# Attention for two heads at a time: one exponential for both, products with v in blocks of two key tiles, maxima by one transpose, reciprocals in two parts

## The chip, the core and the metric

The kernel runs on one core of one Trainium2 chip. The metric is the device time of one execution in microseconds. PE is the matrix engine (PEld its weight loads), DVE, ACT and POOL are the vector, scalar and general engines, SP issues most DMAs.

## The reference

Two blocks stand one behind the other. The first has two layers of attention over 512 latent tokens and 256 context tokens, width 1024, heads of 64. Each layer has three mixers of eight heads: A attends to all keys, B to a neighbourhood with a bias, C to a window with a sink. Layer 0 also attends from the context tokens; layer 1 doesn't. The second block (a recurrent and a convolution mixer, a conformer, two mixtures of experts) is not touched.

```python
def block(qi):                                   # mixer A; B and C alike, with bias, mask, sink
    s = jnp.einsum('bqhgd,bkhd->bhgqk', qi, k_all)
    p = softmax_f32(s, v_all.dtype)
    return jnp.einsum('bhgqk,bkhd->bqhgd', p, v_all)
...
mod = c_silu @ ada_w + ada_b                     # modulation, for every layer
hx = rmsnorm(x, norm_w) * (1 + scale[:, None, :]) + shift[:, None, :]
ux = jnp.concatenate([ya, yb, yc_], axis=-1) * jax.nn.silu(px[9])
x = x + gate[:, None, :] * (ux @ w_out)
```

## The kernel before

`layer` runs six groups per layer: mixer A's (or C's) two, B's two, C's (or A's) two; a group has four heads in two pairs. `pair` calls `attend` once for the latent queries and, in layer 0, once for the context queries: 24 latent attends and 12 of the context. While a group's pairs run, the projections for the next group (`proj_tok`, `proj_feat`, whose matmuls are lines 159 to 161 and 362 to 364) and the gate of the last are open too. A scheduler sets one fixed order of instructions for each engine from the order of the code and priorities; each engine runs its own in that order.

An attend has these steps, for the pair's two heads i = 0 and 1.

- **Maxima.** Scores with queries on the partitions (lines 698 to 725), reduced along the keys on DVE into `mt`. A matmul with one column of `mt` as weights (line 738), one for each head and each 128 queries, lays them along a row in bank `pr`. ACT copies the row into the operand `q2` (line 740), so that the second score matmul also subtracts the maximum.
- **Scores.** For each tile of 128 keys and each head, `st` writes the transposed scores into a bank "s" of 128x512 (two matmuls, lines 757 and 760; the masks of C between, line 759). There are two such banks.
- **Exponentials.** ACT writes P of 128x512 from the bank (line 813; 788 for the context; for mixer B DVE adds the bias first, line 842, and the exponential is line 843). P has four buffers (`PB`).
- **Sums.** `add` sums P over the key tiles into `acc` of that head (line 776), by turns on DVE and POOL, so that head 0 has DVE and head 1 POOL where a tile makes one add for each.
- **Products with v.** After each key tile `avm` (line 763) multiplies with v, 64 columns of the array for each head, into one bank `av` of 128x512: head 0 on partitions 0 to 63, head 1 on 64 to 127. P and v are full fp32, and each such matmul has two records in the trace. A and C have six key tiles of up to 512 queries (in C 256 or 384 for four of them); B has two of 512 and four of 256.
- **Normalising.** `reciprocals` sums four heads' `acc` over the partitions (line 865) and takes reciprocals on DVE (line 867) into `rs`; `normalise` spreads them with the 0/1 matrix `bsel` (line 876, fp32) and multiplies `y`.

Beside this, `fill` (called once at the end of every projection) advances `adaln_v`, which works out the modulation of later layers on DVE from weights in the ring (lines 243 and 245, 512 or 1024 wide) and sums over the partitions on PE (line 253).

Of the kernel before, what the change touches and what calls it, by code (L numbers as in the profile page):

```python
# [12 lines left out]
F32 = mybir.dt.float32  # L13
# [4 lines left out]
ALU = mybir.AluOpType  # L18
# [30 lines left out]
class K:  # L49
# [179 lines left out]
    def adaln_v(self, z, wsrc, a, b, nv, bias, mod, tmp):  # L229
# [4 lines left out]
        n = 1024 // nv  # L234
        for c0 in range(a, b, n):
            acc = self.t(tmp, [128, 1024], tag="adr", bufs=1)[:].rearrange("p (v n) -> p v n", v=nv)
            for k0 in range(0, 8, 2 * nv):
                w = self.wload(kview(wsrc[k0 * 128:(k0 + 2 * nv) * 128, c0:c0 + n]), 2 * nv, n)
                for k in range(2 * nv):
# [6 lines left out]
                if k0 + 2 * nv < 8:  # L246
                    yield 1
# [100 lines left out]
    def proj_tok(self, wsrc, nk, tiles, evac):  # L348
# [17 lines left out]
        self.fill(1)  # L366

    def proj_feat(self, wsrcs, x, segs, evac, nb=2, kind="b"):
# [22 lines left out]
        self.fill(1)  # L391


    R0 = 6

    def first_block(self):
        nc, A = self.nc, self.A
        with ExitStack() as es:
# [9 lines left out]
            self.bsel = load("bsel", [128, 2, 128])  # L408
# [6 lines left out]
            with self.rings(self.R0, 3), self.banks(a=2, f=2, b=3, x=1):  # L415
                xs = self.new_x()
                with self.pool("fl") as fl, self.pool("ec") as ec:
                    z1, c1 = self.cvec(ec, "cv1", fp)
# [84 lines left out]
    def layer(self, l, eh, norm=None):  # L503
# [5 lines left out]
        with eh, ExitStack() as es:  # L509
            with self.banks(m=2, s=2, av=1, b=3):  # L510
# [172 lines left out]
    def attend(self, mx, seg, hpair, q1, q2, k1, k2, vf, y, l):  # L683
# [7 lines left out]
        mt = self.t(ap, [128, 2, 4], tag="mt", bufs=3)  # L691
# [38 lines left out]
        if mx == 0 and lat:  # L730
            nc.vector.tensor_reduce(mt[:], mp[:], op=ALU.max, axis=AX.X)
# [19 lines left out]
        if lat:  # L751
            acc = [self.t(ap, [128, 512], tag="acc", bufs=4) for _ in range(2)]
        else:
            acc = [self.t(ap, [128, 256], tag="accc", bufs=2) for _ in range(2)]
# [10 lines left out]
        first = [None, None]  # L765
# [1289 lines left out]
```

## Time and profile before

| | |
|---|---|
| Median of three runs | 3079.18 us (3076.28 to 3086.53) |
| The profiled execution's own time | 3082.83 us |
| Its span | 3080.8 us |
| Busy in the span: PE, DVE | 2760.5 us (90%), 1514.0 us (49%) |
| ACT, POOL | 923.3 us (30%), 815.7 us (26%) |
| Mean granted clock of PE | 0.952 |

The durations used are from the one profiled execution. A busy time counts overlapping instructions once. The end of a matmul is modelled, so that a row of PE can reach beyond the start of the next; the distance of two starts is the better price. Where a wait is put down to an engine, it is the one whose signal came last.

### The profile page before, as it was taken

The numbers are of one execution on the slowest core, as the hardware profiler recorded it, in microseconds if no ns is written. First come the engines' busy times: TensorE is split into PE (matmuls) and PEld (weight loads), VectorE is DVE, ScalarE is ACT, GpSimd is POOL, SyncE is SP. The second block draws the span as 40 slices with busy tenths as digits, with TensorE's granted clock in tenths as the row PEclk, the third lists the DMA queues.
The fourth block names the chain that finished last, engine by engine and source line by source line (L and its number), as shares of the span: only waits on it lengthen the run. The fifth ranks groups of instructions, "written<-read, shape, count | busy, mean of one in ns | idle before, by whom it ended". The sixth has DMA issues, their size and how long they took to land.

```text
span 3080.8 us, 36122 instructions
## 1 busy us (share of the span) xinstructions
PE 2760.5 (90%) x14014; PEld 1717.2 (56%) x14014; DVE 1514.0 (49%) x2793; ACT 923.3 (30%) x1651; POOL 815.7 (26%) x689
## 2 busy tenths in 40 slices
PE   6889899999899999999998877998888997998887
PEld 2486567776588666765676764433333665333332
DVE  5886664656625645786356773222124663221222
ACT  3434343443423453434335321101002232110101
POOL 2243233332333334343534660000001431000000
PEclk8999899999899999999999888999999998999999
DMA  9632024222253214421331338999996574999996
GB/s 285 210 124 62 22 87 133 90 73 66 73 164 120 76 54 145 137 89 55 116 97 58 103 116 345 420 421 420 421 420 244 154 271 192 420 420 420 420 421 273
DMA packets 225306, 634.26 MB, mean 206 GB/s; under 512 B 12559, under 2 KB 141591, under 8 KB 175728
## 3 DMA queue, kind: packets, MB, share of 16 engines
q1 hardware_dynamic: 213344, 597.62, 51.7%
q0 software_dynamic: 7312, 25.96, 2.5%
q10 hardware_dynamic: 4480, 8.39, 0.7%
q8 instruction: 110, 1.80, 0.3%
q14 instruction: 60, 0.49, 0.1%
HBM read 612.87 MB, written 19.14 MB: 205 GB/s over the span
## 4 chain that ended last, share of the span: by engine, by line
PE 28%; DMA 19%; DVE 5%; POOL 2%; ACT 2%; issue 1%; SPq 0%; DVEq 0%; ACTq 0%; POOLq 0%
DMA mr<-in_exp_w_dram 10%; PE b L1859 10%; DMA mq<-in_exp_w_dram 8%; PE b L159 4%; PE b L161 4%; PE b L160 3%; PE av L763 1%; PE b L209 1%; PE b L1844 1%; PE q L275 1%; DVE lh L1262 0%; PE s L757 0%; DMA scratch<-sb 0%; PE b L324 0%; DVE f L1473 0%
## 5 line engine op out<-in xcount | busy, mean ns | idle before, releaser
L154 POOL TENSOR_TENSOR wl<-ring,wh 128x512 fp32r<-128x512 f32 x304 | 417.3, 1377 | 676.1 <-ACT wh L153 658.0
L153 ACT CAST wh<-ring 128x512 fp32r<-128x512 f32 x304 | 187.4, 620 | 505.9 <-PE b L161 366.6
L1859 PE MATMUL b<-mr,xs 128*64 128x512 f32 x1216 | 283.7, 617 | 37.2 <-DMA mr<-in_exp_w_dram 28.7
L159 PE MATMUL b<-hh,wh 128*128 128x512 f32 (+1 forms) x800 | 294.9, 369 | 3.0 <-DVE sc L621 3.0
L160 PE MATMUL b<-hh,wl 128*128 128x512 f32 (+1 forms) x800 | 290.6, 363 | 1.3 <-POOL wl L154 1.3
L161 PE MATMUL b<-hl,wh 128*128 128x512 f32 (+1 forms) x800 | 289.4, 363 | 0.1
L1859 PE MATMUL b<-mq,xs 128*64 128x512 f32 x832 | 189.2, 604 | 25.2 <-DMA mq<-in_exp_w_dram 16.8
L1859 PEld LDWEIGHTS b<-mr,xs 128*64 128x64 f32 x1216 | 90.1, 141 | 216.6 <-issue 154.6
L1801 POOL DMA_INDIRECT xg<-scratch,ix x16 | 15.5, 967 | 728.0 <-DVE ix L1795 687.5
L763 PE MATMUL av<-P,kv 128*64 128x512 f32 (+2 forms) x672 | 191.8, 518 | 3.0 <-ACT P L813 1.8
L1859 PE MATMUL b<-mr,sb 128*64 128x512 f32 x704 | 159.4, 597 | 18.5 <-DMA mr<-in_exp_w_dram 18.3
L159 PEld LDWEIGHTS b<-hh,wh 128*128 128x128 f32 x800 | 153.3, 192 | 32.4 <-issue 5.6
L160 PEld LDWEIGHTS b<-hh,wl 128*128 128x128 f32 x800 | 153.2, 192 | 26.9 <-issue 4.3
L161 PEld LDWEIGHTS b<-hl,wh 128*128 128x128 f32 x800 | 152.6, 191 | 25.0 <-issue 4.5
L362 PE MATMUL b<-wh,hh 128*128 128x256 f32 x512 | 148.9, 291 | 2.1 <-DVE kb L1160 1.3
L813 ACT ACTIVATE P<-s 128x512 f32<-128x512 f32 (+2 forms) x224 | 116.7, 551 | 113.8 <-PE s L760 110.0
L363 PE MATMUL b<-wl,hh 128*128 128x256 f32 x512 | 148.3, 290 | 0.3 <-POOL wl L154 0.3
L364 PE MATMUL b<-wh,hl 128*128 128x256 f32 x512 | 147.8, 289 | 0.4 <-DVE hl L345 0.4
L1883 DVE TENSOR_TENSOR yl<-yl,b 128x512 f32<-128x512 f32 x32 | 22.0, 688 | 254.1 <-PE b L1859 254.1
L1859 PEld LDWEIGHTS b<-mq,xs 128*64 128x64 f32 x832 | 60.2, 138 | 146.2 <-issue 101.6
L776 POOL TENSOR_TENSOR acc<-acc,P 128x256 f32<-128x256 f32 (+2 forms) x96 | 99.5, 1039 | 118.2 <-ACT P L813 94.2
L757 PE MATMUL s<-q1l,k 128*128 128x512 f32 (+2 forms) x288 | 113.2, 403 | 2.1 <-DVE sc L802 1.6
(564 smaller groups left out, 5681.4 us busy)
## 6 DMA issues: line engine op xcount, KB each, us to landing
mr<-in_exp_w_dram SPq DMA_DIRECT2D x120, 2048.0 KB
mq<-in_exp_w_dram SPq DMA_DIRECT2D x72, 2048.0 KB
ring<-in_w_mod_dram SPq DMA_DIRECT2D x96, 512.0 KB
ring<-in_w_in_dram SPq DMA_DIRECT2D x96, 512.0 KB
ring<-in_ada_w_dram SPq DMA_DIRECT2D x48, 512.0 KB
ring<-in_w_out_dram SPq DMA_DIRECT2D x32, 512.0 KB
bias<-in_BS_dram POOLq DMA_DIRECT2D x16, 512.0 KB, 3.8
bias<-in_BT_dram POOLq DMA_DIRECT2D x16, 512.0 KB, 4.0
```

Of the source, the lines that this page charges most:

```text
L153: nc.scalar.copy(h, src)
L154: nc.gpsimd.tensor_tensor(l, src, h.bitcast(F32), op=ALU.subtract)
L159: m(out, w[0], x[0], start=start, stop=False, skip_group_check=chk)
L160: m(out, w[1], x[0], start=False, stop=False, skip_group_check=chk)
L161: m(out, w[0], x[1], start=False, stop=stop, skip_group_check=chk)
L362: m(o, hh, wh[:, kk, :], start=(k == 0 and i % 2 == 0), stop=False, skip_group_check=True)
L363: m(o, hh, wl[:, kk, :], start=False, stop=False, skip_group_check=True)
L364: m(o, hl, wh[:, kk, :], start=False, stop=stop, skip_group_check=True)
L757: mm(ps, k1[i][:, kt * 128:kt * 128 + 128], q1[i][:, a:b], start=True, stop=False)
L763: mm(av[64 * i:64 * i + 64, a:b], vf(i, kt), P, start=start, stop=stop)
L813: nc.scalar.activation(p[:, :w], ps[:, :w], AF.Exp)
L1859: mm(ps[hf][64 * e:64 * e + 64, :], lhs(k, e), wt[:, e, k2, hf * 512:hf * 512 + 512], start=k == 0, stop=k == 7)
```

## The change

- **One activation for both heads.** `bank2` gives a tile "d" of 128x1024, two banks of PSUM, one for each head. It has one buffer, in place of the two banks "s". The exponential is one instruction of up to 128x1024 into a P of that size; P has two buffers (`PB` = 2), and `acc` holds both heads, 2 x 512. In mixer B the bias is still added head by head.
- **Sums for both heads in one add**, in turn on DVE and POOL along one chain.
- **Products in blocks.** `products` takes two key tiles and issues four matmuls, the later tile first, heads in turn.
- **Maxima.** `mt` is a view of one of three buffers `mw` of 128x100 that are set to zero once per layer; head 1's columns lie 32 behind head 0's. One transpose per 128 queries brings 96 columns to 96 partitions; the rows are 0 and 32.
- **Reciprocals in two parts.** `bsel` is rounded once (0 and 1), `rs` is split into a rounded part `rh` (ACT) and the rest `rl` (POOL), and `normalise` adds two matmuls of rounded operands in place of one in fp32.
- **Modulation.** `adaln_v` works in units of half the width, and `fill` is called for two (`FILL` = 2) where it was one; in the second block it is one again.

```diff
+    def bank2(self):
+        return self.t(self.psum, [128, 1024], tag="d", bufs=self.caps["d"])[:].rearrange("p (i n) -> p i n", i=2)
...
-        n = 1024 // nv
+        n = 512 // nv
+        nk = 2 * nv
...
-        self.fill(1)
+        self.fill(self.FILL)
...
-            with self.banks(m=2, s=2, av=1, b=3):
+            with self.banks(m=2, d=1, av=1, b=3):
...
+                    self.mw, self.nmw = self.chunks(ap, "mw", 3, 100), 0
+                    for w in self.mw:
+                        nc.gpsimd.memset(w[:], 0.0)
...
-        mt = self.t(ap, [128, 2, 4], tag="mt", bufs=3)
+        mw = self.mw[self.nmw % len(self.mw)]
+        self.nmw += 1
+        mt = mw[:, 0:64].rearrange("p (i t) -> p i t", i=2)[:, :, 0:4]
...
-        for i in range(2):
-            for t in range(nq):
-                mm(pr[64 + 32 * i:65 + 32 * i, t * 128:t * 128 + 128], mt[:, i, t:t + 1], self.ident[:], start=True, stop=True)
+        for t in range(nq):
+            nc.tensor.transpose(pr[0:96, t * 128:t * 128 + 128], mw[:, t:t + 96], self.ident[:])
         for i in range(2):
-            nc.scalar.copy(q2[i][64:65, :], pr[64 + 32 * i:65 + 32 * i, :n])
+            nc.scalar.copy(q2[i][64:65, :], pr[32 * i:32 * i + 1, :n])
...
-        def avm(i, kt, P, a, b, start, stop):
-            mm(av[64 * i:64 * i + 64, a:b], vf(i, kt), P, start=start, stop=stop)
+        def products(items, start=False, stop=False):
+            todo = [(i, *x) for x in reversed(items) for i in range(2)]
+            for j, (i, kt, P, a, b) in enumerate(todo):
+                mm(av[64 * i:64 * i + 64, a:b], vf(i, kt), P[:, i, :], start=start and j < 2, stop=stop and j >= len(todo) - 2)
...
+        def add(P, a, b, first=None):
+            o = acc[:, :, a:b]
+            self.nadd += 1
+            eng = nc.vector if self.nadd % 2 else nc.gpsimd
+            eng.tensor_tensor(o, o if first is None else first, P, op=ALU.add)
...
-        def tile1(kt, a, b, mask=(), start=False, stop=False):
-            Ps = []
-            w = b - a
+        def tile1(kt, a, b, mask=()):
+            ps = self.bank2()[:, :, :b - a]
             for i in range(2):
-                ps = self.bank("s")
-                st(i, kt, ps[:, :w], a, b, mask)
-                p = newP()
-                nc.scalar.activation(p[:, :w], ps[:, :w], AF.Exp)
-                add(i, p[:, :w], a, b)
-                Ps.append(p)
-            for i in range(2):
-                avm(i, kt, Ps[i][:, :w], a, b, start, stop)
+                st(i, kt, ps[:, i, :], a, b, mask)
+            P = newP()[:, :, :b - a]
+            nc.scalar.activation(P, ps, AF.Exp)
+            return kt, P, a, b
+
+        t4, t5 = tile1(4, 0, N), tile1(5, 0, N)
+        add(t5[1], 0, N, t4[1])
+        products([t4, t5], start=True)
...
-        rs = self.t(self.ap, [128, 512], tag="rs", bufs=1)
-        self.nc.vector.reciprocal(rs[:], ps[:])
-        return rs
+        rs = self.scratch()
+        self.nc.vector.reciprocal(rs, ps[:])
+        rh, rl = [self.t(self.ap, [128, 512], F32R, tag=tag, bufs=1) for tag in ("rh", "rl")]
+        self.nc.scalar.copy(rh[:], rs)
+        self.nc.gpsimd.tensor_tensor(rl[:], rs, rh[:].bitcast(F32), op=ALU.subtract)
+        return rh, rl
...
-            mm(bc[:], self.bsel[:, p, :], rs[:], start=True, stop=True)
+            for r in rs:
+                mm(bc[:], self.bsel[:, p, :], r[:], start=r is rs[0], stop=r is rs[1])
...
-    PB = 4
+    PB = 2
```

How this moves PE's instructions is shown at three places. In the rows, `s` and `d` are the score banks, `av` the products, `b` a projection (or the sum of `adaln_v`, from `adr`), `m` a small bank, `hh`, `hl`, `wh`, `wl` the two parts of a projection's operands; the line numbers behind L are those of each version.

Place 1, PE, in the first latent attend of layer 0 (mixer A), where projections of the next group are open. Before:

```order
L763 MATMUL av_529_2153<-P_533_2159,kv_430_1536 64x512
L763 MATMUL av_529_2153<-P_535_2164,kv_430_1536 64x512
L757 MATMUL s_536_2168<-q1l_506_2081,k1_498_2049 128x512
L760 MATMUL s_536_2168<-q2l_508_2083,k2_500_2051 128x512
L757 MATMUL s_538_2174<-q1l_507_2082,k1_498_2049 128x512
L760 MATMUL s_538_2174<-q2l_509_2084,k2_500_2051 128x512
L698 MATMUL m_563_2254<-k1_498_2049,q1c_557_2242 128x256 x2
L161 MATMUL b_826_3228<-hl6_425_1456,wh_837_3319 128x512
L763 MATMUL av_529_2153<-P_537_2171,kv_430_1536 64x512
L763 MATMUL av_529_2153<-P_539_2177,kv_430_1536 64x512
L757 MATMUL s_540_2182<-q1l_506_2081,k1_498_2049 128x512
L760 MATMUL s_540_2182<-q2l_508_2083,k2_500_2051 128x512
```

After, from the last two scores of a tile on:

```order
L769 MATMUL d_542_2204<-q1l_513_2109,k1_504_2076 128x512
L772 MATMUL d_542_2204<-q2l_515_2111,k2_506_2078 128x512
L165 MATMUL b_764_3126<-hl7_427_1459,wh_774_3216 128x512
L163 MATMUL b_765_3127<-hh7_419_1451,wh_774_3216 128x256
L164 MATMUL b_765_3127<-hh7_419_1451,wl_775_3217 128x256
L165 MATMUL b_765_3127<-hl7_427_1459,wh_774_3216 128x256
L258 MATMUL b_779_3269<-one32_4_64,adr_776_3248 128x2 x4
L163 MATMUL b_785_3296<-hh0_412_1444,wh_790_3303 128x512
L778 MATMUL av_534_2175<-P_543_2209,kv_434_1544 64x512 x2
L778 MATMUL av_534_2175<-P_541_2201,kv_434_1544 64x512 x2
L769 MATMUL d_544_2216<-q1l_512_2108,k1_504_2076 128x512
L772 MATMUL d_544_2216<-q2l_514_2110,k2_506_2078 128x512
```

Before, the products of one key tile stand between the scores of two others, with one projection matmul. After, projections and a sum of `adaln_v` stand between a tile's scores and the products, and the products are four.

Place 2, PE, in mixer A's second group of layer 0, where the projections of the next group are already used up. Before:

```order
L763 MATMUL av_707_2858<-P_715_2876,kv_430_1536 64x512
L763 MATMUL av_707_2858<-P_717_2882,kv_430_1536 64x512
L757 MATMUL s_718_2887<-q1l_684_2786,k1_499_2050 128x512
L760 MATMUL s_718_2887<-q2l_686_2788,k2_501_2052 128x512
L757 MATMUL s_720_2893<-q1l_685_2787,k1_499_2050 128x512
L760 MATMUL s_720_2893<-q2l_687_2789,k2_501_2052 128x512
L698 MATMUL m_742_2963<-k1_499_2050,q1c_736_2948 128x256 x2
L763 MATMUL av_707_2858<-P_719_2890,kv_430_1536 64x512
L763 MATMUL av_707_2858<-P_721_2896,kv_430_1536 64x512
```

After:

```order
L753 MATMUL m_701_2908<-ident_2_60,mw2_433_1540 96x128
L769 MATMUL d_687_2853<-q1l_657_2757,k1_505_2077 128x512
L772 MATMUL d_687_2853<-q2l_659_2759,k2_507_2079 128x512
L769 MATMUL d_687_2853<-q1l_658_2758,k1_505_2077 128x512
L772 MATMUL d_687_2853<-q2l_660_2760,k2_507_2079 128x512
L778 MATMUL av_679_2824<-P_688_2858,kv_434_1544 64x512 x2
L778 MATMUL av_679_2824<-P_686_2850,kv_434_1544 64x512 x2
L769 MATMUL d_689_2865<-q1l_657_2757,k1_505_2077 128x512
L772 MATMUL d_689_2865<-q2l_659_2759,k2_507_2079 128x512
L769 MATMUL d_689_2865<-q1l_658_2758,k1_505_2077 128x512
L772 MATMUL d_689_2865<-q2l_660_2760,k2_507_2079 128x512
```

Before, a tile's products stand between the scores of the tiles around it. After, two tiles' scores (d_685 ended just above, then d_687) stand next to each other but for one transpose, and the products of both behind them.

Place 3, PE, at the end of layer 1's attention: line 865 (866 after) sums the last heads, line 876 (881) spreads the reciprocals. Before, the end of the gate's projection and the last sum of `adaln_v` lie between them; the last three and the ones around are:

```order
L161 MATMUL b_2827_13075<-hl7_1854_8540,wh_2837_13129 128x512
L159 MATMUL b_2828_13076<-hh7_1846_8532,wh_2837_13129 128x512
L160 MATMUL b_2828_13076<-hh7_1846_8532,wl_2838_13130 128x512
L161 MATMUL b_2828_13076<-hl7_1854_8540,wh_2837_13129 128x512
L253 MATMUL b_2843_13159<-one32_4_64,adr_2663_12474 128x2 x8
L876 MATMUL m_2825_13065<-rs_2824_13063,bsel_12_79 128x512
L876 MATMUL m_2826_13068<-rs_2824_13063,bsel_12_79 128x512
L159 MATMUL b_2888_13254<-uh0_2844_13170,wh_2892_13260 128x512
```

After:

```order
L778 MATMUL av_2491_12401<-P_2504_12455,kv_2205_11042 64x512 x2
L778 MATMUL av_2491_12401<-P_2502_12447,kv_2205_11042 64x512 x2
L866 MATMUL m_2524_12560<-acc_2492_12402,two_13_80 32x512 x2
L881 MATMUL m_2528_12571<-rh_2526_12567,bselr_12_79 128x512
L881 MATMUL m_2528_12571<-rl_2527_12568,bselr_12_79 128x512
L881 MATMUL m_2529_12575<-rh_2526_12567,bselr_12_79 128x512
L881 MATMUL m_2529_12575<-rl_2527_12568,bselr_12_79 128x512
L163 MATMUL b_2591_12760<-uh0_2547_12676,wh_2595_12766 128x512
```

The fifteen projection matmuls and the sum that stood between the two steps have moved up, and the spreading follows the sums directly, with four matmuls in place of two.

## Rows read from the trace of the kernel before

**Rows 1.** Busy time by engine, both layers: span, PE, PEld, DVE, ACT, POOL, clock, DMA, GB/s

```profile
230.00:1490.00 1260.00, 1202.54 (x6559) 860.43 (x6558) 748.20 (x1377) 520.65 (x956) 451.48 (x410) 0.97 0.29 91
```

**Rows 2.** Waits from 230 to 1490 us: total us, times, longest us

```profile
ACT P L813 <- PE s L760: 110.0, 84, 2.5
...
PEld s L757 <- issue: 80.0, 110, 1.6
...
PEld av L763 <- ACT P L813: 47.3, 146, 1.8
```

**Rows 3.** Time line of PE: start us, us, engine, line, operation, count

```profile
386.70 0.40 PE L760 MATMUL s<-q2l,k 65*128 65x512 f32 x1
...
387.17 0.40 PE L760 MATMUL s<-q2l,k 65*128 65x512 f32 x1
...
387.40 0.40 PE L698 MATMUL m<-k,q1c 128*128 128x256 f32 x2
...
387.78 1.60 PE L763 MATMUL av<-P,kv 128*64 128x512 f32 x4
...
389.32 0.50 PE L757 MATMUL s<-q1l,k 128*128 128x512 f32 x1
...
258.69 1.08 PE L763 MATMUL av<-P,kv 128*64 128x512 f32 x4
...
259.70 0.50 PE L757 MATMUL s<-q1l,k 128*128 128x512 f32 x1
```

**Rows 4.** Groups by form on PE, 230 to 1490 us: busy us, mean ns

```profile
L763 PE MATMUL av<-P,kv 128*64 128x512 f32 x320 | 115.9, 627 | 2.7 <-ACT P L813 1.8
...
L763 PE MATMUL av<-P,kv 128*64 128x256 f32 x288 | 57.4, 398 | 0.4 <-ACT P L788 0.2
...
L738 PE MATMUL m<-ident,mt 128*1 128x128 f32 x480 | 48.0, 282 | 6.0 <-DVE mt L733 4.5 <-DVE mt L731 1.5
...
L876 PE MATMUL m<-rs,bsel 128*128 128x512 f32 x48 | 24.6, 622 | 3.0 <-DVE rs L867 2.4 <-DVE k L668 0.6
...
L763 PE MATMUL av<-P,kv 128*64 128x384 f32 x64 | 18.5, 512 | 0.0
```

**Rows 5.** Time line of ACT at the same tile

```profile
387.13 1.13 ACT L813 ACTIVATE P<-s 128x512 f32<-128x512 f32 x2 [0.71 <-PE s L760]
```

**Rows 6.** Groups by form on ACT, whole span

```profile
L813 ACT ACTIVATE P<-s 128x512 f32<-128x512 f32 x160 | 89.1, 597 | 79.7 <-PE s L760 77.1 <-POOL wl L154 1.4 <-PE m L706 0.2
...
L667 ACT CAST k<-raw 64x768 fp32r<-64x768 f32 x16 | 13.4, 835 | 2.8 <-PE s L757 2.6
...
L1247 ACT ACTIVATE lsq<-lsq 128x1024 f32<-128x1024 f32 x4 | 4.3, 1064 | 0.8 <-DVE lsq L1244 0.8
```

**Rows 7.** Time line of PE, four transposes

```profile
612.28 0.79 PE L965 MATMUL m<-ident,sc 128*128 128x128 f32 x4 [1.84 <-ACT sc L962]
```

**Rows 8.** Groups by form on POOL, whole span

```profile
L154 POOL TENSOR_TENSOR wl<-ring,wh 128x512 fp32r<-128x512 f32 x304 | 417.3, 1377 | 676.1 <-ACT wh L153 658.0 <-issue 8.2 <-DMA ring<-in_w_mod_dram 5.8
...
L1463 POOL TENSOR_TENSOR S<-S,K 128x1024 f32<-128x1024 f32 x4 | 13.7, 3420 | 3.0 <-DVE t L1462 3.0
...
L1456 POOL TENSOR_TENSOR t<-C,K 128x1024 f32<-128x1024 f32 x4 | 10.5, 2636 | 0.0
```

**Rows 9.** Time line at the end of layer 1

```profile
1472.45 3.36 DVE L867 RECIPROCAL rs<-m 128x512 f32<-128x512 f32 x1 [2.34 <-PE m L865]
...
1476.58 0.61 ACT L153 CAST wh<-ring 128x512 fp32r<-128x512 f32 x1
```

**Rows 10.** Groups by form on DVE, whole span, the modulation units

```profile
L245 DVE SCALAR_TENSOR_TENSOR adr<-ring,cv2s,adr 128x1024 f32<-128x1024 f32 x49 | 70.3, 1434 | 60.7 <-DMA ring<-in_w_mod_dram 60.3
...
L245 DVE SCALAR_TENSOR_TENSOR adr<-ring,cv1s,adr 128x512 f32<-128x512 f32 x56 | 48.2, 903 | 3.8 <-DMA ring<-in_ada_w_dram 3.7
```

**Rows 11.** Busy time by engine as in rows 1, two stretches with the granted clock

```profile
373.70:383.90 10.20, 7.46 (x27) 4.03 (x26) 4.31 (x10) 1.06 (x2) 0.00 (x0) 0.50 0.00 0
...
384.00:411.30 27.30, 26.05 (x120) 13.12 (x120) 12.36 (x21) 17.69 (x37) 8.98 (x8) 1.00 0.00 1
```

More of the change, by code (lines that the diff above doesn't have):

```diff
@@ L750, in attend @@
         av = self.bank("av")
[L751 to L754, printed above, removed]
+        acc = self.t(ap, [128, 2, n], tag="acc" if lat else "accc", bufs=2 if lat else 1)
         def st(i, kt, ps, a, b, mask=()):
@@ L795, in attend @@
-            for t in range(2):
-                for i in range(2):
-                    avm(i, 4 + t, P[i][:, t * C:t * C + C], 0, C, t == 0, t == 1)
-            pss = self.bank("s")
+                    st(i, 4 + t, ps[:, i, t * 256:t * 256 + 256], 0, C)
+            P = newP()
+            nc.scalar.activation(P, ps, AF.Exp)
+            add(P[:, :, 0:C], 0, C, P[:, :, C:2 * C])
+            if mx == 2:
+                sinks()
+            products([(4 + t, P[:, :, t * C:t * C + C], 0, C) for t in range(2)], True, True)
@@ L799, in attend @@
+            pss = self.bank("m")
             for i in range(2):
-                mm(pss[64 * i:64 * i + 64, :n], self.two[:], acc[i][:], start=True, stop=True)
+                mm(pss[64 * i:64 * i + 64, :n], self.two[:], acc[:, i, :], start=True, stop=True)
             rs = self.scratch()
@@ new lines, in tile1 @@
+            P = newP()[:, :, :b - a]
+            nc.scalar.activation(P, ps, AF.Exp)
+            return kt, P, a, b
+        t4, t5 = tile1(4, 0, N), tile1(5, 0, N)
+        add(t5[1], 0, N, t4[1])
+        products([t4, t5], start=True)
+        if mx != 1:
+            for k0 in (0, 2):
+                items = []
+                for kt in (k0, k0 + 1):
+                    a, b, mask = 0, N, []
+                    if mx == 2:
+                        a, b = max(0, (kt - 1) * 128), min(N, (kt + 2) * 128)
+                        if kt > 0:
+                            mask.append((0, 0))
+                        if kt < 3:
+                            mask.append((b - a - 128, 256))
+                    items.append(tile1(kt, a, b, mask))
+                    add(items[-1][1], a, b)
+                products(items, stop=k0 == 2)
@@ L848, in attend @@
+                nc.scalar.activation(P, P, AF.Exp)
+                items = []
                 for j in range(2):
                     a = self.BW[j0 + j]
-                    for i in range(2):
-                        avm(i, j0 + j, Ps[i][:, j * 256:j * 256 + 256], a, a + 256, False, j0 + j == 3)
+                    items.append((j0 + j, P[:, :, j * 256:j * 256 + 256], a, a + 256))
+                    add(items[-1][1], a, a + 256)
+                products(items, stop=j0 == 2)
         if mx == 2:
@@ L856, in attend @@
         if mx == 2:
-            for i in range(2):
-                nc.vector.tensor_tensor(acc[i][es[i], :], acc[i][es[i], :], e[es[i], :], op=ALU.add)
-        return acc
+            sinks()
+        return [acc[:, i, :] for i in range(2)]
     def reciprocals(self, sums):
@@ L864, in reciprocals @@
         for j, acc in enumerate(sums):
[L865 to L868 removed]
+            self.nc.tensor.matmul(ps[32 * j:32 * j + 32, :], self.two[:, 0:32], acc, start=True, stop=True)
+        rs = self.scratch()
[4 more added lines that the diff above has]
+        return rh, rl
     def normalise(self, mx, ys, rs):
```

75 lines of the change are left out of this document (22 added, 53 removed).

## The prediction

> **What bounds the kernel now.** I read the stretches first. The two attention layers lie between 230 and 1490 us, and there PE is busy for 1202.5 of 1260 us [rows 1]; behind them nothing is edited and PE's order is row for row the same, so a microsecond of PE saved in the layers should shift all the rest. The waits come next. ACT waits 110.0 us for scores, in 84 stops; it is nearly always free when they come. The other way round, PE's weight loads for the products with v stop 146 times for the exponentials, 47.3 us in all, and the loads for the scores behind the products wait another 80.0 us for nothing but PE itself [rows 2]. So I then read one key tile on PE. In the tile at 386 us the four score matmuls start about 0.24 us apart (386.70 to 387.17 is two), and the products follow at 387.78 and hold PE until 389.32, that is 1.54 us. The same four records at 258.69 take until 259.70, that is 1.01 us [rows 3]. The work is equal. At 258.69 both heads' exponentials were there, and the halves of the array (64 columns to each head) ran side by side; at 387.78 the second head's exponential came some 0.5 us after the first's, because ACT takes the heads one by one. About 80 such pairs of 512 columns stand in the layers; by their busy time they cost 115.9 / 80 = 1.45 us, near the late case [rows 4].
>
> **Products.** One activation releases both heads together, and a block has two key tiles, so the halves run together throughout. A matmul's two records are 0.48 us each at 512 columns (1.01 us for two in a row and 0.05 us to leave). Place 1 in the order shows the block of four matmuls: 4 x 0.48 + 0.05 = 1.97 us, where two late pairs took 3.08. In busy time (the modelled end adds some 0.1 us to each group) the three widths sum to 115.9 + 57.4 + 18.5 = 191.8 us now [rows 4]. After: 80 pairs x 0.96, 72 x 0.48 and 16 x 0.72 make 122.9, and 84 groups x 0.15 make 12.6, in all 136 us: **-56 us**. The groups (runs of L763 in PE's time line) fall from about 161 to 84, and each costs 0.15 us before its first product (387.40 plus two of 0.11 to 387.78, [rows 3]): **-11 us**. Bounds: -35, if half of the pairs were in fact already side by side, and -75.
>
> **Waits for scores.** The price of this is the one buffer d. Where two banks took turns, a score tile now waits until the activation has read the last. From rows: 386.70 to 387.13 from the last score matmul to the activation, 0.43 us; the activation; 0.05 us to the next PE instruction (387.13 + 0.60 to 387.78) [rows 3, 5]. No activation of 128x1024 from PSUM stands in the trace; the nearest is 1.064 us for 1024 from SBUF, and 2 x 0.597 bounds it above [rows 6]. I take 1.06, as 0.835 for 768 and 0.597 for 512 lie on that line. Less the matmul's own 0.24 us, PE has 1.3 us to cover behind each 1024-wide tile, some 1.1 behind 768 and 0.95 behind 512. In 18 of the 24 latent attends the order covers this with projections: place 1 has a 512-wide matmul, three of 256, the four of L253 and one more of 512 between the scores and the products, over 1.3 us. I count 0.1 us left over at five gaps: **+9 us**. In the other six nothing is there to put between (place 2): both pairs of mixer A's second group in layer 0, three attends of mixer C in layer 0, and the very last attend. Adding up the order: 8.6 us uncovered in each of the first two, 7.3 in each of the next three (narrower tiles), 7.1 in the last, and 2 in a half covered one: **+48 us**. So these six lose what the blocks give them. Bounds for both: +40 (shorter reads) to +90.
>
> **Maxima.** 480 records of one column take 48.0 us of PE [rows 4]. Now 4 transposes (2 for the context) replace 16 (8) records. Four transposes took 0.79 us [rows 7], of which I take 0.3 as the modelled end that the next matmul doesn't wait for; so 24 x 0.5 + 12 x 0.25 = 15 us remain: -33, and some 0.1 us for each of 36 changes of the array's shape: **-37 us**. Bounds -25 and -42. The copies to the stacks stay.
>
> **Reciprocals.** 48 records of the spreading matmul are busy 24.6 us [rows 4]. The two parts are rounded operands, one record each of 0.24 us: 48 x 0.24 = 11.5, **-13 us**. The split adds a cast on ACT (0.61 us) and a subtraction on POOL (1.38 us) behind a reciprocal of 3.36 us [rows 8, 9]. In eleven groups the next group's work stands between. In the last, place 3, PE now waits for all of it: before, 15 projections and L253 filled that wait; now they were used earlier. **+5 us**.
>
> **Adds.** 1024-wide adds of both heads take turns on DVE and POOL in one chain. POOL's price is 2.64 us, or 3.42 beside DVE work [rows 8]; two tiles on PE last about 6 us, and one DVE and one POOL add 1.2 + 2.64, so the chain keeps up, also behind one split of 1.38 us. Each P is released by the slower of its add and its block; with slack of some 1.7 us the block is later. 0, bounds -3 and +20. First and second head's adds no longer run side by side: the trace has 2.64 and 3.42 us for one shape on POOL. The Trainium skill says why that can be (GPSIMD Engine Reference, 1. Specifications: POOL shares its SBUF interfaces with VectorE, with contention where DVE reads two SBUF inputs); no run here separates it, and by that rule turn-taking adds would be the cheaper ones, so this term would go below 0.
>
> **Modulation units.** Halved in width and called twice per projection: same loads, twice the DVE instructions. By rows, 1.43 us for 1024 against about 0.9 for 512 [rows 10], some 35 us more DVE in a stretch where DVE is busy 748 of 1260 us [rows 1]. In return no single one blocks DVE as long. 0, bounds 0 and +12. ACT loses 140 activations, about 20 us of a queue that waits for PE: 0.
>
> **Sum.** -56 - 11 + 9 + 48 - 37 - 13 + 5 = -55 us. Against the profiled execution's 3082.83 that is 3028; the median of the runs lies 3.65 us below that execution, so **3024 us**.
>
> **Rivals.** *Late activations (slower side).* One buffer leaves no slack: if a cast of 0.61 us [rows 9] stands ahead of the exponential, PE waits for it. At six gaps in each of 18 covered attends that is 108 x 0.61 = 66 us, net +11: 3090. It decides from 0.5 us per gap. For it: ACT's queue holds casts for projections between the exponentials, and covers are as long as the wait and no longer. Against: ACT is busy 521 of 1260 us and waited for PE, not PE for it [rows 1, 2]. Chance 0.15.
> *The add chain.* If POOL's adds queue behind two splits each (2 x 1.38 + 2.64 + 1.2 = 6.6 us for two tiles of 5.9), P comes free late by 0.7 us, 60 times: 42 us, 3066. POOL is free for two thirds of the stretch; chance 0.09.
> *No side by side.* If the second head still starts one record behind the first although both operands are there (the change doesn't do what it says), a block takes five records in a row, 5 x 0.48 + 0.05 = 2.45 us: that gives back 0.48 us in each of 40 wide blocks and half of it in 44 narrow ones, some 30 us: 3054. Against it the row at 258.69; chance 0.05.
> *The clock.* The granted clock fell to 0.50 at 373.7 us, where PE waited on maxima, and was 1.00 from 384, over scores with short waits [rows 11]; these are the 1.2 and 2.4 GHz levels. If the longer waits in the six uncovered attends let it fall, about 13 us of matmuls in each double: +78, 3102. The Trainium skill has such a rule (TensorE: Matmul & The Clock Gate, A second HAM failure mode: psum-queue depth-cycling): PE idling briefly between groups that cycle through PSUM lets the clock swing. By that rule, 3102; the stretch from 384 us, which has a wait in every tile, does not bear it out. Chance 0.04.
>
> **How the numbers follow.** Forecast 0.67; rivals 0.15, 0.09, 0.05, 0.04. The forecast's own range, from the bounds, is 2990 to 3052. To leave out no more than 2 in 10 the range takes in the add chain and half of the late activations: 2992 to 3074. About 0.3% (9 us) is what a measurement of this kernel can tell from no change. Faster: 0.67 + 0.07 + 0.05 + 0.02 = 0.81; the same: 0.08; slower: 0.11, mostly late activations.
>
> **What would show it.** After the change, the products should be busy near 136 us against 191.8, the transposes near 15, PE should wait for exponentials in whole steps of about 1.3 us in six attends and by tenths elsewhere, and the second block should have its old length. Wrong it would be if waits of PE for the exponentials sum to over 100 us, if POOL's adds release them, or if the clock reads 0.50 in scores and products.

## The result

| | time, us | ratio to before, 95% interval |
|---|---|---|
| before | 3080.65 (3076.28 to 3086.53) | |
| after | 3110.39 (3107.72 to 3113.92) | 1.0095 (1.0082 to 1.0109) |

The change makes the kernel 30 us slower; 55 us faster was forecast. The profiled execution of after has a span of 3112.1 us against 3080.8. All but 4 of these 31 us arise in the two attention layers: the first matmul behind layer 1 starts at 1510.1 us, before at 1482.7.

PE does less and waits more. Busy time by engine in the kernel after (columns as in [rows 1]): both layers, mixer A's second group in layer 0, and a stretch of it.

```profile
230.00:1490.00 1260.00, 1129.12 (x6165) 834.84 (x6165) 771.25 (x1419) 504.97 (x814) 436.05 (x352) 0.93 0.27 89
321.00:461.00 140.00, 102.73 (x389) 62.48 (x382) 70.13 (x130) 43.59 (x72) 31.12 (x22) 0.73 0.07 22
336.20:370.30 34.10, 21.59 (x49) 11.56 (x50) 18.13 (x32) 8.43 (x14) 4.17 (x4) 0.50 0.00 0
```

PE is busy 1129 us of 1260, 73 less than in [rows 1], though layer 1 is not at its end there by 1490. The same group before, from 306 to 407 us, was 39 us shorter at a granted clock of 0.92:

```profile
306.00:407.00 101.00, 90.75 (x411) 54.62 (x407) 57.60 (x109) 43.77 (x88) 29.68 (x28) 0.92 0.06 17
```

The groups on PE (columns as in [rows 4]) that answer to it, and the new activation on ACT (as in [rows 6]):

```profile
L778 PE MATMUL av<-P,kv 128*64 128x512 f32 x308 | 87.7, 696 | 9.0 <-ACT P L818 8.8
...
L778 PE MATMUL av<-P,kv 128*64 128x256 f32 x288 | 42.5, 406 | 10.2 <-ACT P L800 7.8 <-ACT P L818 2.2
...
L753 PE MATMUL m<-ident,mw 128*96 128x128 f32 x120 | 21.7, 296 | 7.6 <-DVE mw L748 2.9 <-DVE mw L746 2.7 <-DVE mw L715 1.6
...
L778 PE MATMUL av<-P,kv 128*64 128x384 f32 x64 | 13.8, 511 | 1.3 <-ACT P L818 1.3
...
L818 ACT ACTIVATE P<-d 128x1024 f32<-128x1024 f32 x80 | 82.1, 1026 | 94.5 <-PE d L772 86.7 <-DVE acc L785 7.2
```

So these parts do what they should: the products are busy 144 us (forecast 136, before 191.8), the activation takes 1.03 us (estimate 1.06). The waits (as in [rows 2]) show what the change brought with it:

```profile
ACT P L818 <- PE d L772: 134.4, 77, 6.0
...
DVE acc L785 <- POOL acc L785: 51.8, 14, 8.2
...
PEld d L769 <- issue: 41.4, 53, 1.6
...
PEld d L769 <- ACT P L818: 32.0, 45, 2.3
...
PEld m L721 <- DVE mp L722: 19.4, 23, 4.0
...
PE d L769 <- ACT P L818: 16.2, 17, 2.0
```

Summed by the engine that ended them, PE's own waits from 227 us to the end of layer 1 (PEld's, which run beside them, left out) are 46 us before and 79 after for DVE, 6 and 53 for ACT, 0 and 6 for POOL. So only part of the new idle time is the wait for exponentials that was forecast.

These sums don't show which step of PE's work became longer, because matmuls overlap. So I added up PE's time line from the start of each matmul to the start of the next: waits then belong to the matmul ahead of them, and the sums close. Groups 1 to 6 are layer 0's, cut at the matmuls of `reciprocals` (lines 865 and 866); "projections" has the modulation's small matmuls in it; the last column is time at clock 0.50. Before, then after, in us:

| | length | scores | products | maxima | projections | at 0.50 |
|---|---|---|---|---|---|---|
| 1 (A) | 79, 94 | 15.2, 14.7 | 17.0, 14.0 | 7.7, 8.1 | 31.3, 52.2 | 0, 5 |
| 2 (A) | 102, 140 | 16.6, 30.8 | 20.2, 20.5 | 16.6, 32.6 | 33.0, 34.5 | 17, 77 |
| 3 (B) | 118, 92 | 12.0, 10.7 | 12.9, 10.5 | 5.6, 5.3 | 75.0, 58.7 | 7, 0 |
| 4 (B) | 124, 114 | 11.6, 11.2 | 12.9, 10.5 | 6.0, 5.4 | 83.3, 80.3 | 3, 0 |
| 5 (C) | 78, 90 | 14.9, 21.4 | 14.8, 14.0 | 6.3, 7.9 | 32.3, 34.5 | 0, 14 |
| 6 (C) | 88, 97 | 17.8, 28.6 | 14.8, 15.8 | 12.2, 18.4 | 24.3, 19.1 | 24, 42 |
| both layers | 1256, 1283 | 157, 198 | 181, 143 | 87, 112 | 683, 705 | 82, 190 |

The row of group 1 is the key. Its scores cost no more than before, since projections fill the gaps that the one buffer opens: 52 us of them stand there, 21 more than before. They were not made for that; they are taken from what follows. In group 2 they are missing where they were needed. The 34.5 us in its row hide this, so I counted records: before, 139 of the projections' matmuls stand in group 2 ahead of the end of its first pair's maxima; after, 63, the last at 336.6 us, and then none up to 441 us. PE's time line there, with the wait ahead of an instruction in brackets:

```profile
332.17 0.40 PE L163 MATMUL b<-hh,wh 128*128 128x512 f32 x1
334.88 0.30 PE L912 MATMUL m<-ident,raw 128*128 128x128 f32 x1 [2.31 <-DVE raw L902]
...
341.76 0.47 PE L912 MATMUL m<-ident,raw 128*128 128x128 f32 x1 [3.33 <-DVE raw L902]
...
347.50 0.80 PE L721 MATMUL m<-k,q1l 128*128 128x512 f32 x1 [0.57 <-DVE mp L722]
348.10 0.41 PE L724 MATMUL m<-k,q1l 128*128 128x256 f32 x1
349.08 0.80 PE L721 MATMUL m<-k,q1l 128*128 128x512 f32 x1 [0.57 <-DVE mp L722]
```

From 332.6 us PE waits for DVE's rotation of the heads, the granted clock goes to 0.50 at 336.2, and the maxima then step at 1.58 us (347.50 to 349.08) with nothing else between. In the kernel before the same steps took 1.29 us (337.23 to 338.52), and projections stood between them:

```profile
337.23 0.50 PE L706 MATMUL m<-k,q1l 128*128 128x512 f32 x1
337.57 0.39 PE L160 MATMUL b<-hh,wl 128*128 128x512 f32 x1
337.81 0.28 PE L709 MATMUL m<-k,q1l 128*128 128x256 f32 x1
337.92 0.39 PE L161 MATMUL b<-hl,wh 128*128 128x512 f32 x1
338.15 0.28 PE L159 MATMUL b<-hh,wh 128*128 128x256 f32 x1
338.27 0.28 PE L160 MATMUL b<-hh,wl 128*128 128x256 f32 x1
338.38 0.28 PE L161 MATMUL b<-hl,wh 128*128 128x256 f32 x1
338.52 0.50 PE L706 MATMUL m<-k,q1l 128*128 128x512 f32 x1
```

Two things in these rows are not the missing projections. The step itself is longer because its matmul takes 0.80 us at 0.50 where it took 0.50 at the full clock: in group 1 of the changed kernel, at the full clock, the steps from 283.9 to 289.0 us take 1.25 to 1.29 us. The 14 steps of group 2 at 0.50 pay some 4 us for that, out of the 16 by which its maxima grew. And the wait of 3.33 us ahead of 341.76 is group 1's reciprocal, which DVE now takes in the middle of the rotation; before, it came ahead of it (DVE, after and before):

```profile
338.00 3.36 DVE L868 RECIPROCAL sc<-m 128x512 f32<-128x512 f32 x1
...
306.69 3.36 DVE L867 RECIPROCAL rs<-m 128x512 f32<-128x512 f32 x1 [3.15 <-PE m L865]
```

The projections' +22 us in the last row of the table have another place: in layer 0 they sum to 279 us before and after. In layer 1, 18 steps from one of their matmuls to the next matmul last over 0.8 us, 38 us in all; before there were 10, with 19 us. Most of them end with DVE, 11 us of idle time with the gate (line 634) and 5 us with the bias of mixer B, which is read from the one buffer (line 846). Ahead of the longest wait for the gate (4.65 us) DVE works 4.91 us on four instructions of a modulation unit.

### The profile page after: what moved, and what is told of

Read it like the earlier page. It is cut to its first block, busy times and chain, and to the rows that moved or that the text cites. A ratio compares the mean times of both kernels' runs of the same rounds, so it can differ in the third digit from the quotient of the medians.

```text
span 3112.1 us, 35133 instructions
## 1 busy us (share of the span) xinstructions
PE 2699.1 (87%) x13654; PEld 1697.8 (55%) x13654; DVE 1547.5 (50%) x2867; ACT 915.8 (29%) x1524; POOL 816.7 (26%) x641
## 4 chain that ended last, share of the span: by engine, by line
PE 42%; DMA 18%; DVE 10%; ACT 4%; POOL 3%; issue 3%; SPq 0%; DVEq 0%; POOLq 0%; ACTq 0%
PE b L1865 11%; DMA mr<-in_exp_w_dram 9%; DMA mq<-in_exp_w_dram 8%; PE b L163 6%; PE b L165 6%; PE b L164 6%; PE av L778 2%; PE d L769 1%; DVE adr L250 1%; PE d L772 1%; ACT P L818 1%; PE b L1850 1%; PE b L213 1%; PE b L367 1%; PE b L369 1%
## 5 line engine op out<-in xcount | busy, mean ns | idle before, releaser
L1865 PE MATMUL b<-mq,xs 128*64 128x512 f32 x832 | 187.7, 600 | 26.8 <-DMA mq<-in_exp_w_dram 18.4
L778 PE MATMUL av<-P,kv 128*64 128x512 f32 (+2 forms) x672 | 144.1, 552 | 21.6 <-ACT P L818 13.4
L818 ACT ACTIVATE P<-d 128x1024 f32<-128x1024 f32 (+2 forms) x112 | 104.7, 935 | 146.8 <-PE d L772 138.9
L785 POOL TENSOR_TENSOR acc<-acc,P 128x512 f32<-128x512 f32 (+2 forms) x48 | 86.5, 1802 | 232.6 <-ACT P L818 198.5
L769 PE MATMUL d<-q1l,k 128*128 128x512 f32 (+2 forms) x288 | 116.8, 410 | 26.3 <-ACT P L818 17.4
## 6 DMA issues: line engine op xcount, KB each, us to landing
mq<-in_exp_w_dram SPq DMA_DIRECT2D x72, 2048.0 KB, 32.6
```

The source lines that it names most:

```text
L769: mm(ps, k1[i][:, kt * 128:kt * 128 + 128], q1[i][:, a:b], start=True, stop=False)
L778: mm(av[64 * i:64 * i + 64, a:b], vf(i, kt), P[:, i, :], start=start and j < 2, stop=stop and j >= len(todo) - 2)
L818: nc.scalar.activation(P, ps, AF.Exp)
L1865: mm(ps[hf][64 * e:64 * e + 64, :], lhs(k, e), wt[:, e, k2, hf * 512:hf * 512 + 512], start=k == 0, stop=k == 7)
```

## The experiments

Each block of runs shares its runs of the kernel before, whose medians lie between 3079.4 and 3082.4 us.

### Which part costs: taking edits back

*The additions* go back to one engine for each head:

```diff
...
-            eng = nc.vector if self.nadd % 2 else nc.gpsimd
-            eng.tensor_tensor(o, o if first is None else first, P, op=ALU.add)
+            for i, eng in enumerate((nc.vector, nc.gpsimd)):
+                o = acc[:, i, a:b]
+                eng.tensor_tensor(o, o if first is None else first[:, i, :], P[:, i, :], op=ALU.add)
```

> The changed kernel, but each head's sums of exponentials are added up on an engine of their own again (VectorE head 0, GpSimd head 1, halves of the same tiles), so that no addition waits for the other engine's. Theory A (one score buffer: TensorE stands between the scores of one tile and the next, and its granted clock falls to 0.50 in stretches without a projection): the additions are not the cause, the time stays within 10 us of the changed kernel's 3110 and about 141 us of layer 0 stay at clock 0.50. Theory B (the chain of additions that changes engine at every step holds VectorE up for 52 us and the maxima and rotations behind it): 3065 to 3085, and VectorE's waits for GpSimd's additions fall from 52 us to under 5. Theory C (the halved modulation units and the order they leave): 3105 to 3115.

Measured 3111.9 us, ratio 1.0097 (1.0074 to 1.0120): theory B falls. The 51.8 us that DVE waited for POOL were slack. Theories A and C both allow this time.

*The activations* go back to two banks "s" and one activation for each head (blocks stay):

```diff
...
-            ps = self.bank2()[:, :, :b - a]
...
             for i in range(2):
-                st(i, kt, ps[:, i, :], a, b, mask)
-            nc.scalar.activation(P, ps, AF.Exp)
+                ps = self.bank("s")
+                st(i, kt, ps[:, :b - a], a, b, mask)
+                nc.scalar.activation(P[:, i, :], ps[:, :b - a], AF.Exp)
```

> The changed kernel with two one-bank score buffers and one activation for each head, as before the change; products in blocks of two tiles, the additions over both heads at once, the transposes, the split reciprocals and the modulation units stay as changed. Theory A: the waits at the scores go and most of the loss with them, 3045 to 3075, and the time at clock 0.50 in layer 0 falls from 141 us to 60 to 90. Theory B: within 10 us of 3110. Theory C: 3105 to 3115.

Measured 3078.6 us, 0.9993 (0.9981 to 1.0004), and 78 us at clock 0.50 in layer 0 (139 in the changed kernel): A holds in direction; the time lies 4 us above its range.

*Both edits together:*

> Both of the two edits together: scores and activations for each head and additions for each head as before the change, while the products in blocks, the transposes, the split reciprocals and the halved modulation units stay. Theory A: as in the run with the activations of each head alone, 3040 to 3070, since the products (56 us), the group leads (11 us) and the maxima (37 us) are kept. Theory B: 5 to 10 us under the run with the additions of each head alone. If both count, it is below each of them by about what the other gains. Theory C: still above 3090.

Measured 3069.9 us, 0.9962 (0.9950 to 0.9975). With per-head additions, the one buffer with its common activation costs 3111.9 - 3069.9 = 42 us; the additions count 9 us here and -1.5 behind the one buffer.

*Without the blocks too*, which leaves maxima, split and modulation units on the kernel before:

> The kernel before with three of the parts: the maxima by transposes, the reciprocals in two parts and the halved modulation units; scores, activations, products and additions as before. By the prediction's terms -37 -8 +0 = -45 us, 3035. Theory C (the modulation units or the order that they leave cost time, or the maxima's 37 us lie in time that something else fills): 3075 or more. Theories A and B both expect it below 3060, since neither cause is in it.

Measured 3079.5 us, 0.9995 (0.9983 to 1.0006): 44 us from the sum of the prediction's terms, with neither A nor B in it. So C is true as well: something in these three parts takes away what the maxima give.

### One part alone

*The maxima*, the `mw` part of the diff:

> The kernel before with one part alone: the maxima turned by transposes of 96 columns. By the prediction's term 37 us less, 3044. If TensorE's time in the layers is set by waits for VectorE and ScalarE that the 480 one-column records only filled: 3074 to 3084.

Measured 3059.9 us, 0.9937 (0.9920 to 0.9953). The change's best part, 20 us of the forecast 37. Start to start, its 120 transposes take 16.3 us where 480 records took 44.5; the products next to them grow from 181 to 190.

*More of the old maxima.* Line 738 is issued twice:

> The kernel before with every one-column matmul of the maxima issued twice, so 480 records more (start to start they took 44.5 us in the layers before). If TensorE's work bounds the layers, as the prediction had it: about 3125. If such work is filled into waits that are there anyway: under 3095.

Measured 3141.9 us, 1.0198 (1.0181 to 1.0215), that is +62 for 480 short records, 0.13 us each, more than the 45 expected. So added work on PE does lengthen the layers, also the smallest; what the parts lack isn't lost because PE's work counted for nothing.

*One activation* on the kernel before (`bank2`, P of 128x1024; additions and products as they were):

> The kernel before with one part alone: one buffer of two banks for the scores and one activation for both heads; additions and products head by head and tile by tile as before. Theory A (the one buffer costs by itself): 42 us more than before, as between the runs of the changed kernel with one and with two banks, 3115 to 3130. If it costs only beside the blocks of two tiles: under 3095.

Measured 3134.1 us, 1.0179 (1.0162 to 1.0196), +54. Start to start, products fall from 181 to 146 us without any block, so the pairing comes from the common activation; scores grow by 41, maxima by 21 and projections by 9, and group 2 has the shape that it has in the changed kernel:

```profile
319.00:464.00 145.00, 105.66 (x432) 62.47 (x431) 75.79 (x136) 43.78 (x75) 35.40 (x27) 0.75 0.08 27
```

*More matmuls where PE waits*, on the changed kernel, for the clock:

```diff
+            if mx == 0 and l == 0 and hpair >= 4:
+                extra = self.bank("m")
+                for _ in range(4):
+                    mm(extra[:], k1[0][:, 0:128], q1[0][:], start=True, stop=True)
...
+                    for _ in range(3 if mx == 0 and l == 0 and hpair >= 4 else 1):
                         mm(ps[:], qs, k1[i][:, 0:N], start=True, stop=True)
```

> The changed kernel with work added in mixer A's second group of layer 0 alone: its 512-wide matmuls for the maxima are issued three times, and four matmuls of 512 columns into a bank that nobody reads stand behind each score tile's activation; 80 matmuls of some 0.24 us, 19 us of TensorE, laid where it waits. If the granted clock is a part of the loss there: the stretches at 0.50 between 319 and 450 us shrink from some 75 us to under 40 and the time doesn't rise, 3095 to 3110. If only the waits count and the clock costs nothing: 3115 to 3130.

Measured 3131.4 us, 1.0161 (1.0144 to 1.0178), 21 above the changed kernel. The clock of the group, which now lies from 318.3 to 473.2 us, did not rise (0.73 without the edit):

```profile
318.30:473.20 154.90, 123.83 (x475) 80.96 (x471) 71.26 (x130) 43.89 (x74) 31.02 (x22) 0.74 0.07 23
```

So this doesn't separate the clock's share: the added matmuls ran at 0.50 too, and lengthened the steps that they were to fill (the group's maxima take 44 us start to start in place of 33).

*The modulation units*, `adaln_v` and `FILL` of the diff:

> The kernel before with one part alone: the modulation units of half the width, two of them after each projection. The maxima alone gave 3060; together with the units and the split reciprocals it was 3079.5, so these two cost 20 us. Theory U (the units: twice the instructions on VectorE, in the way of the maxima and rotations): 3092 to 3102. Theory R (the split: a cast and a subtraction more between the reciprocal and the spreading): 3076 to 3085.

Measured 3105.2 us, 1.0086 (1.0069 to 1.0102), +26: theory U, and above its range. On DVE (columns as in [rows 10]) the two large forms are now

```profile
L246 DVE SCALAR_TENSOR_TENSOR adr<-ring,cv2s,adr 128x512 f32<-128x512 f32 x98 | 94.2, 961 | 42.1 <-DMA ring<-in_w_mod_dram 40.7
L246 DVE SCALAR_TENSOR_TENSOR adr<-ring,cv1s,adr 128x256 f32<-128x256 f32 x112 | 58.7, 556 | 0.1
```

against 70.3 and 48.2 us: the prediction's 35 us of DVE are there. PE's waits for DVE in the layers grow by 17 us, most of the +26. *With the split:*

> The kernel before with the halved modulation units and the reciprocals in two parts. If the 20 us don't hang on the maxima: 3095 to 3105. By the prediction's terms (-8 and 0): 3073. What this run has above the run with the units alone is the price of the split.

Measured 3095.4 us, 1.0056 (1.0039 to 1.0073): the split takes 10 us off, 2 more than forecast.

### Do the parts add up?

*Maxima and split, units of whole width:*

> The kernel before with the maxima by transposes and the reciprocals in two parts (the low part in a scratch tile); modulation units, scores, activations, additions and products as before. If the split's 10 us add to the 20 us of the maxima: 3045 to 3053. If the split only gave back some of what the halved units took: 3057 to 3065.

Measured 3058.8 us, 0.9924 (0.9908 to 0.9941): 1 us under the maxima alone (each against its own runs of before, 24 and 20 us). So most of the split's 10 us exist only beside the halved units.

*Maxima and blocks*, per-head activations, no units and no split:

> The kernel before with the maxima by transposes and the products in blocks of two key tiles; two score buffers, activations and additions for each head, reciprocals and modulation units as before. If the parts add up (the blocks gave 10 us where the units and the split were in it): 3045 to 3055. If the 20 us of the units and the split appear only without the blocks: 3065 to 3075.

Measured 3062.7 us, 0.9949 (0.9932 to 0.9966), 3 us above the maxima alone and between the two expectations. Without a common activation the blocks are worth nothing: products fall by 20 us start to start, scores grow by 15 and maxima by 6.

*The changed kernel with whole units:*

> The changed kernel with the modulation units of whole width, one after each projection, as before the change (the low part of the reciprocals lies in a scratch tile to make room). On the kernel before, the halved units alone cost 25 us; together with the split 15, with the maxima too 20, and beside the blocks 7. If they cost by their work on VectorE whatever else is there: 3085 to 3095. If they cost less where TensorE waits for the one score buffer anyway: 3100 to 3108.

Measured 3109.1 us, 1.0094 (1.0077 to 1.0111). The units that cost 26 us by themselves cost 1 in the changed kernel. That is a balance: with whole units layer 1 is 19 us shorter (PE waits 27 us for DVE there, with halved units 42, before 23), and layer 0 is 16 us longer (47 us of such waits, with halved units 37).

### The buffer or the activation?

A bank now holds both heads' scores for half of the queries, so that the common activation has two buffers. On the changed kernel:

```diff
...
+            w = b - a
+            h = w if w <= 256 else w // 2
+            for c in range(0, w, h):
+                ps = self.bank("s")[:, :2 * h].rearrange("p (i n) -> p i n", i=2)
+                for i in range(2):
+                    st(i, kt, ps[:, i, :], a + c, a + c + h, [(off - c, mo) for off, mo in mask if c <= off < c + h])
+                nc.scalar.activation(P[:, :, c:c + h], ps, AF.Exp)
```

> The changed kernel with the one buffer of two banks replaced by two of one bank: both heads' scores for half of the queries in each, two activations of 2x256 for a tile of 512; all other parts as changed. If the one buffer costs the 42 us: 3060 to 3080, and the time at clock 0.50 in layer 0 under 90 us against 140. If not: 3100 or more.

Measured 3075.4 us, 0.9978 (0.9969 to 0.9988): two buffers bring 35 us back, with the pairing kept (products 142 us). With them come shorter activations (half of the queries) and, in mixer B, one for each head, so the run prices the one buffer with its long activation, not the number of buffers alone. Group 2 is 129 us long, against 141, and the projections are back in it: 131 of their matmuls stand ahead of the end of its first pair's maxima. The clock was missed: layer 0 has 111 us at 0.50, not under 90, and both layers 151, 69 more than before, in a kernel that is 7 us faster than before: the time at the low clock does not set the time of the kernel by itself.

The count of projections goes with the buffer in every run. With the one buffer (the changed kernel and four other runs) group 1 holds 250 to 275 of their matmuls, and 51 to 63 are left ahead of the end of group 2's first maxima. In the fifteen kernels with two buffers, before among them, it is 166 to 219 and 95 to 157.

*The same buffers on the maxima alone, products tile by tile:*

> The kernel before with the maxima by transposes, and one activation for both heads but with two buffers: a bank holds both heads' scores for half of the queries, so a tile of 512 queries takes two activations of 2x256; mixer B's window tiles stay head by head, products tile by tile, reciprocals and units as before. If the one buffer is what the common activation pays for: 3030 to 3062, with the products at 140 to 170 us from start to start against 189.5 with the maxima alone. If the common activation itself is the price (the second head's scores are issued before anything can be read): 3090 or more.

Measured 3093.9 us, 1.0040 (1.0028 to 1.0053), 34 above the maxima alone, against the expectation of the buffer theory. Products fall by 32 us, scores grow by 48 and projections by 13. My reading, which no run isolates: with a product behind every tile PE must wait for both heads' exponential each time, where head by head it could begin with the first. So tile by tile the common activation costs 34 us even with two buffers, and the +54 above are not the buffer's alone; with blocks two buffers helped.

*And with late products:*

> The run with the halves of queries, and each tile's products issued behind the scores of the next tile. Now both heads come from the same activation, so that the products stay in pairs (80 pairs of 512 in the order, where the late products head by head fell apart into single heads). If late exponentials are what the products wait for: 15 to 35 us under the run with the halves. If TensorE meets the same waits at the scores: within 10 us of it.

Measured 3082.9 us, 1.0004 (0.9994 to 1.0013): 11 us better, with the products at 147.5 us: less than the 15 to 35 expected.

*Late products head by head, on the maxima alone:*

> The kernel before with the maxima by transposes, and each key tile's products issued behind the next tile's scores in place of ahead of them, so that both heads' exponentials are there without one common activation; all else as before. If the products cost 181 us from start to start because the second head's exponential comes late: 140 to 155 us, and 3020 to 3035. If their length has another cause, or the delay is paid at the buffers of P: 3055 to 3075.

Measured 3099.7 us, 1.0062 (1.0045 to 1.0079), 40 above the maxima alone and outside both expectations. The order broke the pairs up: 103 stretches on PE hold one head's two records (median 1.00 us at full clock) where before 21 did and 109 held both heads' four (median 1.32 us). Where the two exponentials are released apart, the scheduler put scores between the products of the two heads.

*Both repairs on the changed kernel*, two buffers and whole units:

> The changed kernel with both repairs: two score buffers with halves of the queries, and the modulation units of whole width. If the two prices add: the run with the halves (3075) less 7 to 20, so 3055 to 3068, no better than the kernel before with the maxima alone (3060). If the units cost nothing there: 3070 to 3080.

Measured 3078.3 us, 0.9990 (0.9979 to 1.0001): no addition either. The fastest kernels found are the maxima alone and with the split, 3060 and 3059 us.

## Why the prediction was wrong

Start to start in both layers, after less before, beside the prediction's terms:

| | predicted | measured |
|---|---|---|
| products, with their leads | -67 | -38 |
| scores | +57 | +40 |
| maxima's transposes | -37 | -26 |
| spreading | -13, +5 | +1 |
| the maxima's own matmuls | 0 | +25 |
| projections, modulation | 0 | +22 |
| all else in the layers | 0 | +3 |
| sum | -55 | +27 |

**The step that failed is the cover under "Waits for scores".** I counted projections between scores and products as if they were free there. Their effect on the spot was right: outside groups 2, 5, 6 and layer 1's last two the scores cost 2.5 us less than before (+9 was forecast), and in those five 43 more (+48). But PE has only so many projections. Those that fill group 1's gaps are missing in group 2, where they had hidden DVE's rotation and the paced maxima: the maxima grow by 16 us there, the largest part of the +25. The counts show it (139 matmuls ahead of the end of its first maxima before, 63 after, 131 with two buffers), and so does the time that two buffers bring back (35 us). The +22 of the projections is not this: it lies in layer 1, and with whole units the projections there take 410 us instead of 426 (404 before). So most of it comes with the halved units, which I had priced at 0.

**Products.** The pairing is right: a block of four matmuls of 512 columns takes 1.87 us from its start to the next instruction's at the full clock (1.97 forecast), 143 us in sum. It falls short where the clock is low, since the same block takes 3.61 us at 0.50 (after, at either level):

```profile
1312.43 1.94 PE L778 MATMUL av<-P,kv 128*64 128x512 f32 x8
1314.30 0.39 PE L769 MATMUL d<-q1l,k 128*128 128x256 f32 x1
...
365.75 3.68 PE L778 MATMUL av<-P,kv 128*64 128x512 f32 x8
369.36 0.80 PE L769 MATMUL d<-q1l,k 128*128 128x512 f32 x1
```

In the five groups named above the products lose 6 us of 81, in the others 32 of 100. The eight wide blocks that ran at 0.50 in whole or in part cost 13 us more than at the full clock. And it isn't the blocks that bring it, as one activation alone has it.

**The clock** was the rival nearest in time (3102, chance 0.04). Its sign appeared, 190 us at 0.50 in place of 82, yet in maxima and rotations as much as in scores and products. The Trainium skill (TensorE: Matmul & The Clock Gate, A second HAM failure mode: psum-queue depth-cycling) puts such swings down to short idle times between groups of matmuls that cycle through banks; the trace agrees that the clock swings (0.50 from 336.2 to 370.3 us). Its price can be estimated from rows at both levels: 13 us in the blocks, 4 in the paced maxima and some 5 in the scores, whose matmuls start 0.43 us apart in place of 0.24; in all some 20 to 25 of the 82 us between forecast and result. The prediction's price was 78, because it let 13 us of matmuls double in each of six attends. So the rival holds in part, as a consequence of the waits; no run changes the clock alone, and this share stays an estimate.

**The other signs.** PE's waits for exponentials sum to 36 us (PEld's beside them to 68), not over 100, and POOL's adds release almost none of them; so the late activations and the add chain are not what was missed. The second block is 4 us longer.

**Maxima.** -37 was mis-sized. In the run of the maxima alone 16.3 us remain (15 forecast), but the records had taken 44.5 us start to start and not 48 and their changes of shape, and of the 28 us saved 20 arrive: the products are 8 us longer there.

**Reciprocals.** -8 was right beside the halved units (-10), and -1 without them. **Adds.** 0 holds (-1.5), with 9 us inside the bounds once two buffers are there. **Modulation units.** 0, with 12 as the upper bound, was wrong by itself (+26): a DVE that is half idle still made PE wait, 17 us more in the layers. Inside the change 0 came out right (1) by luck: 19 us lost in layer 1 and 16 gained in layer 0, neither of them forecast. Why layer 0 gains is open.

## What to carry to other kernels

Work that hides a wait can be spent once: before you price a new gap at nothing because independent matmuls stand in it, find where they stood before and what they hid there. Price parts in the company that they will have: here 26 us became 1 and 10 became 1 as other parts came in, and a part that is good alone (the maxima, 20 us) vanished in the whole. Here a buffer taken from the loop between PE and ACT cost more than the common activation saved, though independent work stood in the loop.

## What was not expected of the hardware

- 480 more records of matmuls with one weight column cost 62 us, 0.13 us apiece, where the group of 480 is busy for 48.0 us in the profile [rows 4].
- Halving a DVE instruction from 1024 to 512 columns saves a third of its mean, 1434 to 961 ns [rows 10] (medians 1285 and 752), so that the same work costs 94 us in place of 70.
- 80 added matmuls in mixer A's second group did not lift its mean granted clock (0.73 and 0.74).
- A block of four products, two for each half of the array, takes 1.87 us at the full clock and 3.61 at 0.50.
